# Summing four of six conditioning vectors on GpSimd instead of VectorE

## The chip, the core and the metric

The kernel runs on one core of a Trainium2 chip. A core has TensorE (matrix products, into PSUM), VectorE and ScalarE (elementwise work on SBUF and PSUM), GpSimd (elementwise work on SBUF alone) and SyncE, whose queue SP issues the loads and stores. Each engine runs its own instructions in order and waits for the others by semaphores. The metric is the device time of one execution in microseconds (us), as the median of several runs; lower is better.

## What is computed

One decoder block over 256 tokens of width 2048 in float32, conditioned on one vector c. Six vectors of 2048 numbers come from c by one product with a weight of 2048 x 12288 (100 MB, which is loaded once); the rest of the block uses them as shifts, scales and gates:

```python
c_act = jax.nn.silu(c)
mod = c_act @ w_ada[l] + b_ada[l]
sh_m, sc_m, gt_m, sh_f, sc_f, gt_f = [m[:, None, :] for m in jnp.split(mod, 6, axis=-1)]
h = rmsnorm(x, g[0]) * (1.0 + sc_m) + sh_m
y = token_mixer(h, w_in[l], ...)          # retention and S5 branches, merged by gates, times w_out
x = x + gt_m * rmsnorm(y, g[1])
h = rmsnorm(x, g[2]) * (1.0 + sc_f) + sh_f
y = swiglu_ffn(h, w_ffn_in[l], w_ffn_out[l])
x = x + gt_f * rmsnorm(y, g[3])
```

## The kernel before

**The weight stream.** Every large product goes through `linear`: it walks over pieces of 256 rows by 512 columns of a weight. For each piece SP loads a tile `raw` (L268, 512 KB), ScalarE rounds it to `hi` (L271), VectorE subtracts to get `lo` (the helper `tt`, L80), and TensorE makes twelve matmuls of 512 columns from it (L283, L284, L287: two token tiles, three products, two k-tiles). `raw` has a ring of five buffers (`RB`), `hi` and `lo` have three each. Results are evacuated some pieces later (`defer`).

**The conditioning vectors.** `ada_acc` makes one half of a vector (1024 columns): it loads 16 tiles `araw` of 128 x 1024 and sums them, each times its own element of `cT`, into a tile `acc`: the first by a scaling (L198), the others by a multiply and add in one VectorE instruction (L200). A matmul then sums over the partitions. `acc` has one buffer. The two vectors that the first stretch needs, SC_M and SH_M, are made with `first=True` and take their tiles from a pool of their own, `firstp`. The other four are SC_F and SH_F (`ada_f`, needed by the feed forward), GT_M (`ada_gm`) and GT_F (through `ada_rows`). Their `araw` tiles come from the ring of `raw`, which they share with the weights, but for GT_M, which has five buffers of its own (`lraw`).

**The order.** These sums are generators in a lane, `ada`; after each weight piece `tick` advances the lane by its rate (0.35 pieces' worth, then 0.5 for SC_F and SH_F, 0.8 for GT_M, 0.7 for GT_F). A second lane, `mix`, advances the retention heads and the S5 part in the same way. A scheduler in the language's tile framework may still move an instruction a little within its engine's row. In the profile, SC_F and SH_F are summed from 237 to 733 us, GT_M from 735 to 852, GT_F from 1401 to 1549; the feed forward's first product lies in between.

**GpSimd** has little to do before: memsets, and small powers (`rstd_of`, L140) for norms: `grs` in each retention head, which VectorE's `gnb` (L797) waits for, `rstd` and `rpost` in the other norms. Each S5 group has a small memset of `mg` (L677).

Of the kernel before, what the change touches and what calls it, by code (L numbers as in the profile page):

```python
# [15 lines left out]
ALU = mybir.AluOpType  # L16
# [36 lines left out]
def hybrid_block(ctx: ExitStack, tc: tile.TileContext, A, out, dbg=None):  # L53
# [7 lines left out]
    x_in, w_ada, w_in = A["x"], A["w_ada"], A["w_in"]  # L61
    w_ret, w_glu, w_out, w_f1, w_f2 = A["w_ret_out"], A["w_s5_glu"], A["w_out"], A["w_ffn_in"], A["w_ffn_out"]
    V, S, G, T = nc.vector, nc.scalar, nc.gpsimd, nc.tensor
# [26 lines left out]

# [1 line left out]
    class Lane:  # L92
# [34 lines left out]

# [1 line left out]
    ident = cst.tile([P, P], F32, name="ident")  # L129
# [27 lines left out]
    cT = cst.tile([P, KD], F32, name="cT")  # L157
# [18 lines left out]

# [1 line left out]
    mod = cst.tile([P, 96], F32, name="mod")  # L178
# [8 lines left out]
    def ada_acc(col, n, first=False):  # L187
        acc = adp.tile([P, n], F32, tag="acc", name="acc")
        for kt in range(KD):
# [6 lines left out]
            nc.sync.dma_start(raw, w_ada[kt * P:(kt + 1) * P, col:col + n])  # L196
            if kt == 0:
                V.tensor_scalar(acc, raw, cT[:, 0:1], None, op0=ALU.mult)  # L198
            else:
                V.scalar_tensor_tensor(acc, raw, cT[:, kt:kt + 1], acc, op0=ALU.mult, op1=ALU.add)  # L200
            yield acc
# [62 lines left out]

# [1 line left out]
    def split_piece(w, k0, KP, c0, keep=None, kept=None, tag="hi", hi=None):  # L266
# [94 lines left out]

# [1 line left out]
    def square_sum(a, o):  # L363
# [39 lines left out]

# [1 line left out]
    NS = 32  # L405
# [119 lines left out]

# [1 line left out]
    eye = cst.tile([P, 32], F32, name="eye")  # L527
# [219 lines left out]

# [1 line left out]
    ret = []  # L749
# [51 lines left out]

# [1 line left out]
    KG = [(0, 4), (4, 10), (10, 16)]  # L803
# [113 lines left out]

# [1 line left out]
    flush()  # L919
# [53 lines left out]

# [1 line left out]
    def out_evac(pst, t, n, Y, ssq, Gr, squared=False):  # L975
# [91 lines left out]

# [1 line left out]
    h2 = lhs_of(h2_t)  # L1069
# [87 lines left out]
```

## Time and profile before

| | |
|---|---|
| median of 3 runs | 1674.71 us (1673.17 to 1676.5) |
| span of the profiled execution, first to last instruction | 1672.3 us |
| TensorE matmul busy | 1622.4 us, 97% |
| VectorE busy | 1167.2 us, 70% |
| ScalarE busy | 800.0 us, 48% |
| GpSimd busy | 19.0 us, 1% |
| moved by DMA | 398.14 MB, 238 GB/s |

The profile comes from one execution, of 1672.3 us; the median lies 2.4 us above that span. Busy shares are averages over stretches with different limits, so the stretches in which the four vectors are summed have to be read each by itself. In the rows below PE is TensorE's matmuls, PEld its weight loads, DVE is VectorE, ACT ScalarE, POOL GpSimd, and SPq SyncE's queue; L200 is line 200 of the kernel. An arrow `<-` in a name stands between what an instruction writes and what it reads, and behind a time it names what ended a wait. A tile named `ps_` or `mm` lies in PSUM, the others in SBUF.

### The profile page before, as it was taken

The numbers are of one execution on the slowest core, as the hardware profiler recorded it, in microseconds if no ns is written. First come the engines' busy times: TensorE is split into PE (matmuls) and PEld (weight loads), VectorE is DVE, ScalarE is ACT, GpSimd is POOL, SyncE is SP. The second block draws the span as 40 slices with busy tenths as digits, with TensorE's granted clock in tenths as the row PEclk, the third lists the DMA queues.
The fourth block names the chain that finished last, engine by engine and source line by source line (L and its number), as shares of the span: only waits on it lengthen the run. The fifth ranks groups of instructions, "written<-read, shape, count | busy, mean of one in ns | idle before, by whom it ended". The sixth has DMA issues, their size and how long they took to land.

```text
span 1672.3 us, 20673 instructions
## 1 busy us (share of the span) xinstructions
PE 1622.4 (97%) x7531; PEld 1317.4 (79%) x7531; DVE 1167.2 (70%) x1570; ACT 800.0 (48%) x1102; POOL 19.0 (1%) x39
## 2 busy tenths in 40 slices
PE   5999999999999999999998999999999999999997
PEld 2778887888888888888886788888888888778786
DVE  7878887888878997779967544444444445667554
ACT  4454448454656465544456544444444444334442
POOL 0000000010000000000000000000000000000000
PEclk9999999999999999999999999999999999999999
DMA  9999976865766867799985666666666667889763
GB/s 353 335 316 323 324 236 184 261 198 181 248 222 203 264 205 238 262 317 325 332 282 180 189 188 188 189 189 187 187 187 185 188 189 220 270 284 328 252 190 126
DMA packets 194094, 398.14 MB, mean 238 GB/s; under 512 B 23128, under 2 KB 24488, under 8 KB 193480
## 3 DMA queue, kind: packets, MB, share of 16 engines
q1 hardware_dynamic: 193928, 396.74, 73.7%
q8 instruction: 59, 0.97, 0.2%
q14 instruction: 43, 0.35, 0.1%
q0 software_dynamic: 64, 0.08, 0.0%
HBM read 394.67 MB, written 2.10 MB: 237 GB/s over the span
## 4 chain that ended last, share of the span: by engine, by line
PE 83%; DMA 6%; DVE 5%; ACT 3%; issue 2%; POOL 0%; DVEq 0%; SPq 0%; POOLq 0%; ACTq 0%
PE mm L283 26%; PE mm L287 26%; PE mm L284 26%; DMA araw<-in_w_ada_dram 4%; DVE lo L80 2%; ACT hi L271 1%; DVE acc L200 1%; ACT uS L821 1%; PE ps_v L664 1%; PE ps_ada L183 1%; PE ps_y L709 1%; DMA fraw<-in_w_ada_dram 1%; DMA raw<-in_w_ffn_in_dram 1%; PE ps_a L1090 1%; PE ps_bt L657 0%
## 5 line engine op out<-in xcount | busy, mean ns | idle before, releaser
L271 ACT ACTIVATE hi<-raw 128x1024 fp32r<-128x1024 f32 x539 | 568.4, 1059 | 693.1 <-PE mm L284 581.9
L80 DVE TENSOR_TENSOR lo<-raw,hi 128x1024 fp32r<-128x1024 f32 x519 | 632.2, 1222 | 357.8 <-ACT hi L271 354.1
L283 PE MATMUL mm<-hi,h 128*128 128x512 f32 x1408 | 561.4, 399 | 3.7 <-ACT hi L271 3.4
L284 PE MATMUL mm<-hi,h 128*128 128x512 f32 x1408 | 554.2, 394 | 1.8 <-DVE h L80 1.8
L287 PE MATMUL mm<-lo,h 128*128 128x512 f32 x1376 | 429.4, 393 | 0.8 <-DVE lo L80 0.8
L283 PEld LDWEIGHTS mm<-hi,h 128*128 128x128 f32 x1408 | 266.6, 189 | 61.6 <-ACT hi L271 4.1
L284 PEld LDWEIGHTS mm<-hi,h 128*128 128x128 f32 x1408 | 266.4, 189 | 58.4 <-DVE h L80 2.5
L287 PEld LDWEIGHTS mm<-lo,h 128*128 128x128 f32 x1376 | 258.9, 189 | 61.2 <-DVE lo L80 3.5
L200 DVE SCALAR_TENSOR_TENSOR acc<-araw,cT,acc 128x1024 f32<-128x1024 f32 (+1 forms) x180 | 214.3, 1190 | 58.7 <-DMA araw<-in_w_ada_dram 58.2
L283 PE MATMUL mm<-hi,aT 128*128 128x512 f32 x348 | 136.5, 392 | 0.1
L284 PE MATMUL mm<-hi,aT 128*128 128x512 f32 x348 | 136.4, 392 | 0.0
L287 PE MATMUL mm<-lo,aT 128*128 128x512 f32 x348 | 110.1, 395 | 6.4 <-DVE lo L80 6.3
L287 PEld LDWEIGHTS mm<-lo,aT 128*128 128x128 f32 x348 | 64.3, 188 | 24.4 <-DVE lo L80 11.1
L283 PEld LDWEIGHTS mm<-hi,aT 128*128 128x128 f32 x348 | 65.4, 188 | 15.2 <-ACT hi L271 0.8
L284 PEld LDWEIGHTS mm<-hi,aT 128*128 128x128 f32 x348 | 65.4, 188 | 14.0
L283 PE MATMUL mm<-hi,rT 128*128 128x512 f32 x128 | 51.0, 399 | 0.6 <-ACT hi L271 0.6
L283 PE MATMUL mm<-hi,yg 128*128 128x512 f32 x128 | 50.5, 395 | 0.0
L284 PE MATMUL mm<-hi,mT 128*128 128x512 f32 x128 | 50.5, 394 | 0.0
L284 PE MATMUL mm<-hi,rT 128*128 128x512 f32 x128 | 50.4, 394 | 0.0
L283 PE MATMUL mm<-hi,mT 128*128 128x512 f32 x128 | 50.2, 393 | 0.0
L284 PE MATMUL mm<-hi,yg 128*128 128x512 f32 x128 | 50.1, 391 | 0.0
L287 PE MATMUL mm<-lo,rT 128*128 128x512 f32 x128 | 39.9, 393 | 0.1
(258 smaller groups left out, 1259.5 us busy)
## 6 DMA issues: line engine op xcount, KB each, us to landing
raw<-in_w_ffn_in_dram SPq DMA_DIRECT2D x178, 512.0 KB, 3.7
raw<-in_w_in_dram SPq DMA_DIRECT2D x176, 512.0 KB, 4.7
araw<-in_w_ada_dram SPq DMA_DIRECT2D x128, 512.0 KB, 5.2
raw<-in_w_ffn_out_dram SPq DMA_DIRECT2D x88, 512.0 KB, 5.4
araw<-in_w_ada_dram SPq DMA_DIRECT2D x64, 384.0 KB, 5.6
raw<-in_w_out_dram SPq DMA_DIRECT2D x34, 512.0 KB, 5.8
raw<-in_w_ret_out_dram SPq DMA_DIRECT2D x32, 512.0 KB, 5.1
raw<-in_w_s_glu_dram SPq DMA_DIRECT2D x32, 512.0 KB, 5.0
```

Of the source, the lines that this page charges most:

```text
L80: V.tensor_tensor(o, a, b, op=op)
L183: T.matmul(ps[:, i:i + 1], acc[:, i * P:(i + 1) * P], ones[:, 0:1], start=True, stop=True)
L200: V.scalar_tensor_tensor(acc, raw, cT[:, kt:kt + 1], acc, op0=ALU.mult, op1=ALU.add)
L271: S.activation(hi, raw, AF.Copy)
L283: T.matmul(pst[t], xh, hi[:, k, :], start=kt == ka, stop=False)
L284: T.matmul(pst[t], xl, hi[:, k, :], start=False, stop=False)
L287: T.matmul(pst[t], xh, lo[:, k, :], start=False, stop=kt == kb - 1)
L664: T.matmul(pv[:, o:o + 64], BT[:, ri, t, :], uS[0][:, 4 * e + t, :], start=True, stop=True)
L709: T.matmul(o, X[:, ri, t, :], mat(CB, ri, t), start=ri == 0, stop=False, tile_position=(0, 64 * v))
L821: S.activation(dst, src, AF.Copy)
L1090: T.transpose(ps[:, j * P:(j + 1) * P], act[t][:, j * P:(j + 1) * P], ident)
```

## The change

In `ada_acc`, the accumulations with `first=True` stay on VectorE. In all other calls GpSimd does the work: the first tile is scaled into `acc` by GpSimd, and each further tile is scaled in place by GpSimd and then added to `acc` by a second GpSimd instruction. Comments elsewhere are dropped, with nothing else changed; behind the edit every line number is higher by 5.

```diff
@@ ada_acc
             nc.sync.dma_start(raw, w_ada[kt * P:(kt + 1) * P, col:col + n])
-            if kt == 0:
+            if first and kt:
+                V.scalar_tensor_tensor(acc, raw, cT[:, kt:kt + 1], acc, op0=ALU.mult, op1=ALU.add)
+            elif first:
                 V.tensor_scalar(acc, raw, cT[:, 0:1], None, op0=ALU.mult)
+            elif kt:
+                G.tensor_scalar(raw, raw, cT[:, kt:kt + 1], None, op0=ALU.mult)
+                G.tensor_tensor(acc, acc, raw, op=ALU.add)
             else:
-                V.scalar_tensor_tensor(acc, raw, cT[:, kt:kt + 1], acc, op0=ALU.mult, op1=ALU.add)
+                G.tensor_scalar(acc, raw, cT[:, 0:1], None, op0=ALU.mult)
             yield acc
```

VectorE's row at the first half of GT_M, before: splits `lo` of the weight stream, the gated unit's products `gl`, and the accumulations `acc`.

```order
L80 TENSOR_TENSOR lo_6618<-raw_6614,hi_6616 128x1024
L200 SCALAR_TENSOR_TENSOR acc_6585<-araw_6607,cT_105,acc_6585 128x1024
L80 TENSOR_TENSOR lo_6643<-raw_6639,hi_6641 128x1024
L200 SCALAR_TENSOR_TENSOR acc_6585<-araw_6632,cT_105,acc_6585 128x1024
L200 SCALAR_TENSOR_TENSOR acc_6585<-araw_6675,cT_105,acc_6585 128x1024
L80 TENSOR_TENSOR lo_6661<-raw_6657,hi_6659 128x1024
L200 SCALAR_TENSOR_TENSOR acc_6585<-araw_6696,cT_105,acc_6585 128x1024
L80 TENSOR_TENSOR lo_6682<-raw_6678,hi_6680 128x1024
```

The same place of VectorE's row in the change.

```order
L80 TENSOR_TENSOR lo_6679<-raw_6675,hi_6677 128x1024
L80 TENSOR_TENSOR lo_6705<-raw_6701,hi_6703 128x1024
L80 TENSOR_TENSOR lo_6723<-raw_6719,hi_6721 128x1024
L80 TENSOR_TENSOR gl_6509<-gl_6509,mm_6597 128x512
L80 TENSOR_TENSOR gl_6510<-gl_6510,mm_6598 128x512
L80 TENSOR_TENSOR lo_6745<-raw_6741,hi_6743 128x1024
```

The accumulations are gone from it; the splits and the gated unit's products follow each other as before.

GpSimd's row at the same place of the change. Before, nothing stood there: the last `mg` and the next norm's `rpost` followed each other.

```order
L202 TENSOR_SCALAR araw_6667<-araw_6667,cT_105 128x1024
L202 TENSOR_SCALAR araw_6693<-araw_6693,cT_105 128x1024
L202 TENSOR_SCALAR araw_6737<-araw_6737,cT_105 128x1024
L202 TENSOR_SCALAR araw_6759<-araw_6759,cT_105 128x1024
L205 TENSOR_SCALAR acc_6645<-araw_6646,cT_105 128x1024
L203 TENSOR_TENSOR acc_6645<-acc_6645,araw_6667 128x1024
L203 TENSOR_TENSOR acc_6645<-acc_6645,araw_6693 128x1024
L203 TENSOR_TENSOR acc_6645<-acc_6645,araw_6737 128x1024
L203 TENSOR_TENSOR acc_6645<-acc_6645,araw_6759 128x1024
L202 TENSOR_SCALAR araw_6799<-araw_6799,cT_105 128x1024
L203 TENSOR_TENSOR acc_6645<-acc_6645,araw_6799 128x1024
```

Two passes per loaded tile stand there now; at the head of the half four scalings come ahead of the first write of `acc`, which has to wait until the half before has been read.

GpSimd's row at the first retention heads, before: the powers `grs` of the group norms follow each other.

```order
L140 TENSOR_TENSOR grs_2894<-rst_2895,mhalf_89 128x2
L140 TENSOR_TENSOR grs_2981<-rst_2982,mhalf_89 128x2
L140 TENSOR_TENSOR grs_3009<-rst_3010,mhalf_89 128x2
L140 TENSOR_TENSOR grs_3035<-rst_3036,mhalf_89 128x2
L140 TENSOR_TENSOR grs_3103<-rst_3104,mhalf_89 128x2
```

And the same place in the change.

```order
L202 TENSOR_SCALAR araw_3140<-araw_3140,cT_105 128x1024
L203 TENSOR_TENSOR acc_2116<-acc_2116,araw_3140 128x1024
L140 TENSOR_TENSOR grs_2904<-rst_2905,mhalf_89 128x2
L202 TENSOR_SCALAR araw_3254<-araw_3254,cT_105 128x1024
L203 TENSOR_TENSOR acc_2116<-acc_2116,araw_3254 128x1024
L140 TENSOR_TENSOR grs_2992<-rst_2993,mhalf_89 128x2
L202 TENSOR_SCALAR araw_3314<-araw_3314,cT_105 128x1024
L203 TENSOR_TENSOR acc_2116<-acc_2116,araw_3314 128x1024
L140 TENSOR_TENSOR grs_3020<-rst_3021,mhalf_89 128x2
```

A scaling and an add now stand ahead of a power, and the power waits in the same row for them and for their tile's load.

## Rows read from the trace of the kernel before

**Rows 1.** The page, part 1: busy us, share of the span, instructions.

```profile
PE 1622.4 (97%) x7531; PEld 1317.4 (79%) x7531; DVE 1167.2 (70%) x1570; ACT 800.0 (48%) x1102; POOL 19.0 (1%) x39
```

**Rows 2.** The page, part 4: the chain that ended last, by line.

```profile
PE mm L283 26%; PE mm L287 26%; PE mm L284 26%; DMA araw<-in_w_ada_dram 4%; DVE lo L80 2%; ACT hi L271 1%; DVE acc L200 1%; ACT uS L821 1%; PE ps_v L664 1%; PE ps_ada L183 1%; PE ps_y L709 1%; DMA fraw<-in_w_ada_dram 1%; DMA raw<-in_w_ffn_in_dram 1%; PE ps_a L1090 1%; PE ps_bt L657 0%
```

**Rows 3.** Windows, four stretches: busy us (instructions) by engine, clock, DMA share, GB/s.

```profile
236.00:403.00 167.00, 161.55 (x753) 132.88 (x752) 137.12 (x246) 94.06 (x128) 9.36 (x14) 0.99 0.67 208
403.00:733.00 330.00, 328.70 (x1755) 269.89 (x1754) 275.73 (x428) 190.57 (x353) 0.74 (x7) 1.00 0.75 243
735.00:852.00 117.00, 117.00 (x530) 96.42 (x530) 107.30 (x109) 52.33 (x61) 0.00 (x0) 1.00 0.93 323
1409.00:1550.00 141.00, 135.06 (x584) 107.78 (x583) 97.54 (x86) 56.30 (x63) 0.00 (x0) 1.00 0.87 291
```

**Rows 4.** Waits, 1405 to 1558: us in total, times, longest us.

```profile
PE mm L287 <- DVE lo L80: 5.8, 6, 2.4
```

**Rows 5.** VectorE by line, 735 to 852: xcount | busy us, mean ns | idle before.

```profile
L80 DVE TENSOR_TENSOR lo<-raw,hi 128x1024 fp32r<-128x1024 f32 x40 | 48.7, 1221 | 5.7 <-ACT hi L271 5.6
...
L200 DVE SCALAR_TENSOR_TENSOR acc<-araw,cT,acc 128x1024 f32<-128x1024 f32 x30 | 38.4, 1279 | 0.9 <-DMA araw<-in_w_ada_dram 0.8
...
L80 DVE TENSOR_TENSOR gl<-gl,M 128x512 f32<-128x512 f32 x8 | 5.2, 683 | 0.0
...
L80 DVE TENSOR_TENSOR gl<-gl,Sg 128x512 f32<-128x512 f32 x6 | 3.9, 685 | 0.0
...
L198 DVE TENSOR_SCALAR acc<-araw,cT 128x1024 f32<-128x1024 f32 x2 | 1.5, 746 | 0.0
```

**Rows 6.** VectorE by line, 1409 to 1550.

```profile
L80 DVE TENSOR_TENSOR lo<-raw,hi 128x1024 fp32r<-128x1024 f32 x47 | 57.0, 1222 | 17.3 <-ACT hi L271 17.3
...
L200 DVE SCALAR_TENSOR_TENSOR acc<-araw,cT,acc 128x1024 f32<-128x1024 f32 x29 | 37.2, 1281 | 23.2 <-DMA araw<-in_w_ada_dram 23.0
...
L198 DVE TENSOR_SCALAR acc<-araw,cT 128x1024 f32<-128x1024 f32 x1 | 0.8, 752 | 1.6 <-DMA araw<-in_w_ada_dram 1.6
```

**Rows 7.** VectorE by line, 403 to 733.

```profile
L80 DVE TENSOR_TENSOR lo<-raw,hi 128x1024 fp32r<-128x1024 f32 x100 | 121.2, 1219 | 17.4 <-ACT hi L271 17.3
...
L200 DVE SCALAR_TENSOR_TENSOR acc<-araw,cT,acc 128x1024 f32<-128x1024 f32 x45 | 57.6, 1280 | 28.6 <-DMA araw<-in_w_ada_dram 28.5
...
L80 DVE TENSOR_TENSOR q<-bs,lam 128x256 f32<-128x256 f32 x32 | 12.2, 418 | 0.1
...
L198 DVE TENSOR_SCALAR acc<-araw,cT 128x1024 f32<-128x1024 f32 x3 | 2.2, 745 | 0.0
...
L606 DVE SCALAR_TENSOR_TENSOR cn<-par 128x16 f32<-128x16 f32 x1 | 0.2, 168 | 0.0
```

**Rows 8.** GpSimd by line, whole span.

```profile
L623 POOL MEMSET CB<- 128x1024 f32 x1 | 1.0, 951 | 0.0
...
masks.py:199 POOL TENSOR_SCALAR_AFFINE_SELECT ident<-ident 128x128 f32<-128x128 f32 x1 | 0.3, 296 | 0.0
...
masks.py:197 POOL MEMSET ident<- 128x128 f32 x1 | 0.2, 205 | 0.3 <-POOLq L1143 0.3
```

**Rows 9.** Timeline: start us, us, engine, instruction [idle before <- releaser]; three places.

```profile
357.37 0.68 DVE L80 TENSOR_TENSOR rT<-ps_r,rT 128x512 fp32r<-128x512 f32 x1
357.63 0.69 POOL L140 TENSOR_TENSOR grs<-rst,mhalf 128x2 f32<-128x2 f32 x1 [3.50 <-DVE rst L139]
...
894.72 0.56 POOL L140 TENSOR_TENSOR rpost<-rst,mhalf 128x1 f32<-128x1 f32 x1 [246.24 <-DVE rst L139]
895.31 1.41 DVE L1033 SCALAR_TENSOR_TENSOR x<-Y,rpost,x 128x512 f32<-128x512 f32 x2 [0.67 <-POOL rpost L140]
...
910.83 1.22 DVE L80 TENSOR_TENSOR flo<-raw,hi 128x1024 fp32r<-128x1024 f32 x1
910.99 1.46 POOL L140 TENSOR_TENSOR rpost<-rst,mhalf 128x1 f32<-128x1 f32 x1 [10.85 <-DVE rst L139]
```

**Rows 10.** The page, part 6: DMA issues, KB each, median us to landing.

```profile
araw<-in_w_ada_dram SPq DMA_DIRECT2D x128, 512.0 KB, 5.2
```

## Prediction

> **What bounds the kernel now.** I read the busy shares first: TensorE is busy 97% of the span, VectorE 70%, GpSimd 1% [rows 1]. Then the chain that ended last: three matmul lines hold about 26% each, VectorE's split L80 2%, its accumulation L200 1% [rows 2]. So the matmul stream bounds the kernel nearly everywhere, and VectorE's accumulations are mostly hidden. What the change can win is TensorE's idle time in the stretches where the four vectors are summed. The table of windows gives it [rows 3]: 5.45 us (167 - 161.55) in 236 to 403, 1.3 us in 403 to 733, nothing in 735 to 852, 5.94 us in 1409 to 1550; 12.7 us in all. Only a part of that is VectorE's: in the last stretch the matmuls on lo waited 5.8 us in all for VectorE's split [rows 4].
>
> So the gain is capped at about 6 to 12 us, and the question is whether GpSimd can do the work in the time that each stretch leaves.
>
> **What is removed and added.** By the code eight sums of 16 accumulations leave VectorE: 120 of L200 at 1.28 us and 8 of L198 at 0.75 us [rows 5 to 7], 160 us in all. They stand in four stretches: 48 (45 + 3) in 403 to 733 [rows 7], 32 (30 + 2) in 735 to 852 [rows 5], 30 (29 + 1) in 1409 to 1550 and two just before it [rows 6], and the other 16 in 236 to 403. GpSimd gets two passes over a 128x1024 tile in place of each, a scaling in place and an add that reads two tiles; the add waits for the scaling. I call the pair a step. The time that a stretch has for a step, from its length and its count: 10.4 us in the first, then 6.9, 3.66 and 4.7 us.
>
> **What a step costs.** No row shows either pass at this size. The nearest are GpSimd's memsets: 951 ns for 1024 columns, 205 ns for 128, which makes 0.83 ns a column and 0.1 us fixed; and the select over 128 columns, which also reads its tile, 296 ns, so 91 ns more per 128 columns, 0.73 us per 1024 [rows 8]. Lower bound: each pass is as cheap as a memset, 1.9 us. Upper bound: every read is paid on top, 0.95 + 0.73 for the scaling and 0.95 + 2 x 0.73 for the add, 4.1 us. I choose the memset for the scaling (one tile in, one out) and the row that reads for the add, whose two reads must come through: 0.95 + 2.41 = 3.36 us. The Trainium skill, "GPSIMD Engine Reference", section on performance versus the Vector engine, gives 4497 ns for such an add of 2048 columns; half of that, 2.25 us, is an estimate from that page, and by it the sum below would lose 0.16 us a step, at most 18 us over the 110 steps of the three late stretches.
>
> **What the step meets.** GpSimd's tiny power, one column, takes 0.56 us when VectorE is idle. Started 0.16 us into a VectorE split that reads two SBUF tiles it took 1.46 us, and ended 0.40 us after the split did; started beside a VectorE subtraction that reads one tile from PSUM, it took 0.69 us for two columns [rows 9]. So GpSimd waits for a VectorE instruction with two SBUF inputs, for the whole of it. The Trainium skill, "SBUF", practical consequences of the port table, has the rule: such a pair excludes each other for the full instruction, in either order. The trace agrees for the order seen here; no row shows a long GpSimd read with VectorE behind it. By that rule alone the sum is the full one below; without any exclusion it would be nil.
>
> The VectorE work that stays and reads two SBUF tiles, by stretch: in 735 to 852, lo 48.7, gl with M 5.2 and with Sg 3.9, 57.8 us [rows 5]; in 1409 to 1550, lo 57.0 [rows 6]; in 403 to 733, lo 121.2 and 36 groups of the S5 part from 12.2 down to 0.2 us, 232 instructions and 94.9 us, together 216 [rows 7].
>
> If nothing overlaps, a stretch needs that work plus its steps:
> 735 to 852: 57.8 + 32 x 3.36 = 165.3, against 117: 48 us over. The late ring has five buffers, so GpSimd may lag by five steps less one landing and one step before SP's queue stops: 5 x 3.66 - 5.2 - 3.36 = 9.7 us (landing from [rows 10]). 38 us are left.
> 403 to 733: 216 + 48 x 3.36 = 377, against 330: 47 us.
> 1409 to 1550: 57.0 + 30 x 3.36 = 157.8, against 141: 17 us. The ring here is shared with the weights, so no slack is taken off.
> 236 to 403 has 10.4 us for each step and is taken as free.
> Sum 102 us.
>
> If only the streaming excludes and each instruction's fixed part overlaps, less is lost. From 1221 ns for 1024 columns and about 684 for 512 [rows 5], 0.15 us of a VectorE instruction is fixed; of a GpSimd pass 0.1 us. In 735 to 852: 54 and 64 instructions, 8.1 + 6.4 us off, 24 us left. In 403 to 733: 332 and 96, 49.8 + 9.6 off, 318 us, which fits in 330: nothing. In 1409 to 1550: 47 and 60, 7.1 + 6 off, 4 us. Sum 28 us. I take the middle of 28 and 102, 65 us, less the 2 us or so of waits on lo that VectorE's relief may win back: 63.
>
> **How it reaches the end.** A GpSimd pass that waits holds the next scaling behind it, and with it the araw buffer. SP issues in order, so the next araw load that finds no buffer stops the weight loads behind it; then ScalarE's and VectorE's splits and the matmuls run dry. A split that waits behind an add is late by up to 2.4 us, and its raw buffer with it. No transfer is added: the araw and weight loads are as many as before. The power instructions of the retention (grs) and the memsets of S5 (mg) now stand in GpSimd's row behind steps, as the rows of the program's order show; VectorE's gnb waits for grs. Eight of them, each behind at most one step, are 27 us of VectorE's time at most in 236 to 403, where it is busy 137 of 167 us now [rows 3] and 117 after; I take nothing, since that leaves 50 us idle, and the splits may run three pieces ahead of the matmuls; the price is up to 27 if that cover is gone.
>
> **The rivals.** First, **hidden**: GpSimd's passes overlap VectorE, every step fits (3.36 is below 3.66, the tightest period), nothing is slower and the freed VectorE gives little: 1671 to 1678 us. For it: GpSimd is idle 99% [rows 1]. Against it: the power under the split [rows 9].
>
> Second, **relief** (faster): with accumulations gone, the split comes sooner wherever TensorE waited for it, mostly in 1409 to 1550, where VectorE stands idle 23.2 us before accumulations for araw to land and the split behind them waits too [rows 6]. Price: 6 us there and up to 6 in 236 to 403, 1663 to 1669 us. It decides only if a step under exclusion costs less than (117 + 9.7 - 57.8) / 32 = 2.15 us; the lower bound of 1.9 is below that.
>
> Third, **dear steps**: the upper bound of 4.1 us with full exclusion. 735 to 852: 57.8 + 131.2 - 117 - 9 = 63; 403 to 733: 216 + 196.8 - 330 = 83; 1409 to 1550: 57 + 123 - 141 = 39; sum 185, 1860 us.
>
> Fourth, **the shared ring** alone, without exclusion: in 1409 to 1550 a buffer comes round every 5 x 141 / 77 = 9.2 us (30 accumulations and 47 splits), and an araw tile would hold it 5.2 + 3.36 = 8.6 us. It does not bind by itself, 0 to 5 us, and ends with "hidden".
>
> **How the numbers follow.** The profiled span is 1672.3 us; the median of the runs is 1674.7, so 2.4 us lie around the span. 1672.3 + 63 + 2.4 gives 1738 us. Chances: the forecast (exclusion, 10 to 135 us lost) 0.66; dear steps, or the GpSimd row held up by grs and mg besides, 0.12; hidden 0.12; relief 0.10. About 0.2%, 3.3 us, is what a measurement of this kernel can tell from no change. Of "hidden", 0.11 fall within it and 0.01 below; so faster 0.11, same 0.11, slower 0.78. The range reaches from "hidden" and a part of "relief", 1666, to 1812, which leaves out the dear steps and the rest of relief, some 0.2.
>
> **What would show it.** Right: in the changed kernel's stretches of the GT_M vector and of the S5 part GpSimd is busy most of the time, an add takes well over 2.4 us where it meets a split, lo takes longer than 1.22 us or starts late, SP's loads wait for GpSimd, and TensorE has idle time where it now has none. The first 236 us and the feed-forward part between 950 and 1400 us stay as they are. Wrong: adds of less than 1.5 us, or adds and splits that overlap without stretching; then the time stays or falls. If the loss is in 236 to 403 instead, it is grs and not the port.

## The result, and the profile after

The changed kernel takes 1990.21 us (median of 4 runs, 1986.8 to 1993.27) against 1675.61 us (1673.17 to 1677.5, 4 runs) before: a ratio of 1.1876, 95% interval 1.1855 to 1.1897. The forecast was 1738, with 1812 as its upper end. The direction was right; the loss, 314 us, is five times the 63 that were forecast.

The page of the changed kernel, part 1, the row of TensorE's granted clock in part 2, and the chain of part 4 (before: [rows 1, 2]):

```profile
PE 1728.5 (87%) x7531; PEld 1368.2 (69%) x7531; DVE 1172.6 (59%) x1442; ACT 799.7 (40%) x1102; POOL 767.3 (39%) x287
...
PEclk9999998898989889889978899999999999888999
...
PE 31%; POOL 23%; DMA 10%; DVE 4%; issue 2%; ACT 1%; SPq 0%; POOLq 0%; DVEq 0%; ACTq 0%
```

GpSimd now holds 23% of the chain that ended last, and loads 10%; before, no GpSimd line stood in it. VectorE lost 128 instructions and is busy as long as before: what remains takes longer. TensorE's 7531 matmuls are busy 106 us longer (1728.5 against 1622.4), and TensorE idles 207 us more (257.3 against 49.9).

Where that happens, windows of the changed kernel (columns as in [rows 3]): the retention heads, the end of the S5 part, the sums of GT_M, and the feed forward:

```profile
236.00:403.00 167.00, 128.45 (x539) 102.28 (x538) 104.12 (x138) 69.86 (x92) 86.47 (x32) 0.90 0.49 168
735.00:900.00 165.00, 135.23 (x632) 105.09 (x631) 99.21 (x108) 67.83 (x128) 108.75 (x38) 0.90 0.51 178
900.00:1050.00 150.00, 116.06 (x487) 90.37 (x486) 99.89 (x76) 49.66 (x57) 148.28 (x49) 0.89 0.69 239
1200.00:1650.00 450.00, 450.00 (x2009) 370.20 (x2008) 221.12 (x201) 189.68 (x201) 0.00 (x0) 1.00 0.65 188
```

The last column but two is the granted clock, a mean between its two levels of 1.2 and 2.4 GHz: 0.89 to 0.90 where TensorE has gaps, 1.00 where it has none. In the feed forward nothing changed. In GT_M GpSimd is busy 148 of 150 us; in the two stretches ahead of it only 52% and 66%, and TensorE starves there as well. Those need another reason than a full row.

The costliest groups of part 5 that answer to the step, in the changed kernel (lines are 5 higher):

```profile
L80 DVE TENSOR_TENSOR lo<-raw,hi 128x1024 fp32r<-128x1024 f32 x519 | 702.2, 1357 | 655.8 <-ACT hi L276 645.7
...
L202 POOL TENSOR_SCALAR araw<-araw,cT 128x1024 f32<-128x1024 f32 x120 | 406.9, 3392 | 284.4 <-DMA araw<-in_w_ada_dram 200.1
...
L203 POOL TENSOR_TENSOR acc<-acc,araw 128x1024 f32<-128x1024 f32 x120 | 314.9, 2624 | 9.8
```

A step is 3.39 + 2.62 = 6.0 us, and GpSimd stood idle 200 us for araw tiles that had not landed. The waits of SP's queue in the changed kernel say why they were late (line waited for: us in total, times, longest):

```profile
SPq L196 <- POOL acc L203: 331.8, 54, 10.9
SPq L273 <- POOL acc L203: 321.1, 43, 10.6
```

653 us of loads waited for GpSimd to release a buffer, those of araw (L196) and of weights (L273) alike. One turn of that, SP's queue and then GpSimd, in the changed kernel's S5 part:

```profile
646.14 0.42 SPq L196 DMA_DIRECT2D araw<-in_w_ada_dram  x1
646.65 1.06 SPq L273 DMA_DIRECT2D raw<-in_w_ret_out_dram  x2
658.60 0.34 SPq L196 DMA_DIRECT2D araw<-in_w_ada_dram  x1
```
```profile
651.69 3.87 POOL L202 TENSOR_SCALAR araw<-araw,cT 128x1024 f32<-128x1024 f32 x1 [6.04 <-DMA araw<-in_w_ada_dram]
655.64 2.92 POOL L203 TENSOR_TENSOR acc<-acc,araw 128x1024 f32<-128x1024 f32 x1
662.41 2.85 POOL L202 TENSOR_SCALAR araw<-araw,cT 128x1024 f32<-128x1024 f32 x1 [3.84 <-DMA araw<-in_w_ada_dram]
```

The load issued at 646.14 is there at 651.69; the step ends at 658.56; and at 658.60, not earlier, SP issues the next araw load. GpSimd then idles until that one has landed. So 12.5 us go by for one araw and two weight pieces; SP's queue, which is in order, issues nothing more until 658.60.

To place the loss I take from each trace the first matmul on a split of the gated unit's products `yg`, the first on one of the feed forward's `aT`, and the end of the span. Up to the first lie the sums of SC_F and SH_F, between the two those of GT_M, behind the second those of GT_F. The rows (min/median/max ns, first and last start), before and then after:

```profile
L287 PE MATMUL mm<-lo,aT x348: 388/392/503, 1410.8 to 1663.1; 128*128 128x512 f32 x174
...
L287 PE MATMUL mm<-lo,yg x128: 388/392/397, 720.6 to 812.7; 128*128 128x512 f32 x128
```
```profile
L292 PE MATMUL mm<-lo,aT x348: 387/394/792, 1661.1 to 1976.6; 128*128 128x512 f32 x174
...
L292 PE MATMUL mm<-lo,yg x128: 388/392/796, 899.6 to 1035.2; 128*128 128x512 f32 x128
```

So the loss is 179.0 us with SC_F and SH_F, 71.3 with GT_M (761.5 against 690.2) and 63.2 with GT_F (324.7 against 261.5); together 313.5, the difference of the spans. The same three differences, in us, for the runs below that sum the vectors where the change does; the last column is the time of one run each, but for the change, where it is the median of four. Beside them the kernel before took 1675.1 to 1676.6 us.

| run | SC_F, SH_F | GT_M | GT_F | time |
|---|---|---|---|---|
| the change | 179.0 | 71.3 | 63.2 | 1990.21 |
| e2_shadow | 7.2 | 52.2 | 1.9 | 1735.32 |
| e3_hold | 55.4 | 87.9 | 58.0 | 1875.35 |
| e6_actscale | 79.9 | 32.1 | 14.4 | 1800.62 |
| e7_bcast | 130.4 | 64.1 | 52.9 | 1921.53 |
| e8_noadd | 209.8 | 71.3 | 74.3 | 2029.51 |
| e9_offqueue | 180.2 | 76.2 | 66.1 | 1996.61 |
| e12_write | 8.6 | 40.3 | 24.6 | 1747.55 |
| e14_turns | 155.1 | 72.9 | 56.5 | 1958.55 |
| e15_turns_before | 4.7 | 1.6 | 0.2 | 1680.94 |
| e16_split | 114.6 | 67.4 | 55.8 | 1911.84 |
| e17_split_before | 10.4 | 2.1 | 20.1 | 1707.04 |
| e20_hold_after | 25.9 | 47.7 | 35.7 | 1783.36 |
| e21_hold_split | 32.0 | 39.5 | 35.1 | 1780.65 |

### The profile page after: what moved, and what is told of

Same layout as the page of the kernel before. It is cut to its first block, busy times and chain, and to the rows that moved or that the text cites. A ratio compares the mean times of both kernels' runs of the same rounds, so it can differ in the third digit from the quotient of the medians.

```text
span 1985.8 us, 20782 instructions
## 1 busy us (share of the span) xinstructions
PE 1728.5 (87%) x7531; PEld 1368.2 (69%) x7531; DVE 1172.6 (59%) x1442; ACT 799.7 (40%) x1102; POOL 767.3 (39%) x287
## 4 chain that ended last, share of the span: by engine, by line
PE 31%; POOL 23%; DMA 10%; DVE 4%; issue 2%; ACT 1%; SPq 0%; POOLq 0%; DVEq 0%; ACTq 0%
POOL araw L202 12%; PE mm L288 10%; PE mm L289 10%; PE mm L292 10%; POOL acc L203 10%; DMA araw<-in_w_ada_dram 6%; DMA raw<-in_w_ret_out_dram 2%; DVE lo L80 1%; ACT hi L276 1%; DMA raw<-in_w_ffn_out_dram 1%; POOL acc L205 1%; DMA raw<-in_w_in_dram 1%; DMA raw<-in_w_out_dram 1%; DVE q L80 1%; DMA raw<-in_w_ffn_in_dram 0%
## 5 line engine op out<-in xcount | busy, mean ns | idle before, releaser
L80 DVE TENSOR_TENSOR lo<-raw,hi 128x1024 fp32r<-128x1024 f32 x519 | 702.2, 1357 | 655.8 <-ACT hi L276 645.7
L288 PE MATMUL mm<-hi,h 128*128 128x512 f32 x1408 | 573.2, 407 | 33.1 <-ACT hi L276 32.5
L289 PE MATMUL mm<-hi,h 128*128 128x512 f32 x1408 | 564.0, 401 | 1.7 <-DVE h L80 1.7
L202 POOL TENSOR_SCALAR araw<-araw,cT 128x1024 f32<-128x1024 f32 x120 | 406.9, 3392 | 284.4 <-DMA araw<-in_w_ada_dram 200.1
L203 POOL TENSOR_TENSOR acc<-acc,araw 128x1024 f32<-128x1024 f32 x120 | 314.9, 2624 | 9.8
L205 POOL TENSOR_SCALAR acc<-araw,cT 128x1024 f32<-128x1024 f32 x8 | 29.4, 3675 | 671.0 <-DMA araw<-in_w_ada_dram 486.2
L288 PE MATMUL mm<-hi,aT 128*128 128x512 f32 x348 | 146.1, 420 | 34.1 <-ACT hi L276 34.0
L289 PE MATMUL mm<-hi,aT 128*128 128x512 f32 x348 | 143.4, 412 | 0.0
L288 PE MATMUL mm<-hi,rT 128*128 128x512 f32 x128 | 56.9, 445 | 23.3 <-ACT hi L276 23.2
L288 PE MATMUL mm<-hi,yg 128*128 128x512 f32 x128 | 53.6, 418 | 9.3 <-ACT hi L276 9.3
L198 DVE SCALAR_TENSOR_TENSOR acc<-araw,cT,acc 128x768 f32<-128x768 f32 x60 | 60.9, 1015 | 0.4 <-DMA araw<-in_w_ada_dram 0.2
L288 PE MATMUL mm<-hi,mT 128*128 128x512 f32 x128 | 51.4, 401 | 4.2 <-ACT hi L276 4.2
```

What stands on the lines that cost most here:

```text
L80: V.tensor_tensor(o, a, b, op=op)
L202: G.tensor_scalar(raw, raw, cT[:, kt:kt + 1], None, op0=ALU.mult)
L203: G.tensor_tensor(acc, acc, raw, op=ALU.add)
L205: G.tensor_scalar(acc, raw, cT[:, 0:1], None, op0=ALU.mult)
L288: T.matmul(pst[t], xh, hi[:, k, :], start=kt == ka, stop=False)
L289: T.matmul(pst[t], xl, hi[:, k, :], start=False, stop=False)
```

## The experiments

### What the two passes cost, alone and beside VectorE

The kernel before, with work appended behind its last store: each pass alone, then GpSimd passes and VectorE sums of two SBUF tiles started together.

```diff
+    for n in (1024, 1024, 512, 256):
+        G.tensor_scalar(ga[:, 0:n], ga[:, 0:n], cT[:, 0:1], None, op0=ALU.mult)
...
+        G.tensor_tensor(ga[:, 0:n], ga[:, 0:n], gb[:, 0:n], op=ALU.add)
...
+    for _ in range(8):
+        G.tensor_tensor(ga, ga, gb, op=ALU.add)
+    for _ in range(16):
+        tt(va, va, vb, ALU.add)
```

> The kernel before, with GpSimd passes on dead tiles appended behind the output: first alone, then eight at a time beside VectorE instructions. Its total time is longer by the appended work and says nothing. Theory A (a pass is dear by itself): the scaling of 128x1024 by a per-partition scalar takes about 2.8 us alone, the add about 2.3 us, as the shortest ones in the changed kernel did. Theory B (the passes are stretched by VectorE): alone they take 1.0 to 1.7 us and reach 2.8 only beside VectorE. On exclusion: eight adds beside sixteen VectorE sums of two SBUF tiles (1.22 us each) take 8 x 2.34 + 16 x 1.22 = 38 us together if they exclude each other, 19.5 us if they overlap; beside sums with one PSUM tile, and memsets beside sums of two SBUF tiles, they overlap.

The timeline of GpSimd in that run (start, us): scaling by a column and by a constant, add, multiply by a broadcast column, copy, memset; then 8 adds beside 16 VectorE sums, 8 scalings beside 16 sums, 8 adds beside 32 VectorE sums with a PSUM operand:

```profile
1675.16 2.85 POOL L1141 TENSOR_SCALAR Y<-Y,cT 128x1024 f32<-128x1024 f32 x1
1678.09 2.77 POOL L1142 TENSOR_SCALAR Y<-Y 128x1024 f32<-128x1024 f32 x1
...
1683.88 2.34 POOL L1144 TENSOR_TENSOR Y<-Y 128x1024 f32<-128x1024 f32 x1
1686.30 1.89 POOL L1145 TENSOR_TENSOR Y<-Y,cT 128x1024 f32<-128x1024 f32 x1
1688.25 1.04 POOL L1146 COPY Y<-Y 128x1024 f32<-128x1024 f32 x1
1689.35 0.95 POOL L1147 MEMSET Y<- 128x1024 f32 x1
...
1730.80 26.33 POOL L1153 TENSOR_TENSOR Y<-Y 128x1024 f32<-128x1024 f32 x8
...
1767.62 27.07 POOL L1158 TENSOR_SCALAR Y<-Y,cT 128x1024 f32<-128x1024 f32 x8
...
1795.46 19.33 POOL L1163 TENSOR_TENSOR Y<-Y 128x1024 f32<-128x1024 f32 x8
```

And VectorE's: 8 sums alone, 16 beside the adds, 16 beside the scalings:

```profile
1720.18 10.04 DVE L80 TENSOR_TENSOR Y<-Y 128x1024 f32<-128x1024 f32 x8 [0.28 <-POOL Y L1137]
...
1730.75 36.27 DVE L80 TENSOR_TENSOR Y<-Y 128x1024 f32<-128x1024 f32 x16 [0.28 <-POOL Y L1137]
...
1767.56 26.48 DVE L80 TENSOR_TENSOR Y<-Y 128x1024 f32<-128x1024 f32 x16 [0.28 <-POOL Y L1137]
```

The add is as I had it (2.34 for 2.41; the estimate from the Trainium skill, "GPSIMD Engine Reference", section on performance versus the Vector engine, 2.25, agrees), the scaling three times as dear (2.85 for 0.95): 5.2 us a step. Adds and VectorE's sums shut each other out: 36.27 us, where one after the other would be 18.7 + 20.1. Scalings hardly do: 26.48, not 42.9, some 0.8 us of VectorE's time for each scaling. The rule that I took from the Trainium skill, "SBUF", practical consequences of the port table, thus holds here for the add; for the scaling, which also reads SBUF, the measurement shows no such full exclusion, and decides.

### The port alone, and the hold alone

In `e2_shadow` VectorE keeps all its sums; beside 20 of GT_M's 32 accumulations GpSimd scales and adds a tile that nobody needs. No load of a weight or of an araw tile waits for it.

```diff
+                V.tensor_copy(go, acc[:, 0:1])
+                G.tensor_scalar(scr, scr, go, None, op0=ALU.mult)
+                G.tensor_tensor(scr, scr, scr, op=ALU.add)
```

> The kernel before; VectorE still sums everything, and in the GT_M stretch GpSimd does 20 steps (scaling and add) on a tile of its own, started by a small VectorE copy after the accumulation. No load waits for GpSimd. Theory of the port (GpSimd and VectorE exclude each other): 20 steps of 5.2 us are 104 us, VectorE's two-tile work there is 96 us, the stretch of 117 us grows by 20 to 80 us. Theory of the held buffers: VectorE and GpSimd may wait for each other, but nothing on the path does, and the total grows by less than 10 us.

It took 1735.32 us, 59 more than before: with VectorE's sums still there (107 of 117 us busy, [rows 3]) the passes cost it time that it does not have: the matmuls wait there for VectorE's `lo` and `gl`. Of the 52 us lost with GT_M some 10 have another reason: at the end of the stretch a load of `x` waited 11.7 us for GpSimd's last pass, with the weight loads behind it in SP's queue, and TensorE stood idle 9.9 us in one piece. The rest, some 40 us, lies in the range that I had for the port (20 to 80): where VectorE is full, the port is real.

In `e3_hold` VectorE keeps all its sums too, and GpSimd holds each araw buffer without reading more than two columns of it.

```diff
+            if not first:
+                G.tensor_copy(scr[:, 0:1], raw[:, 0:1])
+                for _ in range(16 if kt else 9):
+                    G.memset(scr, 0.0)
+                G.tensor_copy(scr[:, 0:1], raw[:, 1:2])
```

> The kernel before; VectorE still sums everything, and GpSimd reads one column of each araw tile of the four vectors, then writes 16 memsets of 256 columns (about 5 us, the price of a step) and reads one column again. So every araw buffer is held as long as a GpSimd step holds it, and GpSimd's row is as full, but no long GpSimd read meets VectorE. Theory of the held buffers: 150 to 310 us of the 314 lost come back. Theory of the port: less than 60 us.

1875.35 us, 199 more than before. The small memsets were paced at 0.37 us each, so that the hold came to some 7.2 us and not 6. VectorE's split takes 1223 ns as before, so nothing held it up: holding a buffer and filling GpSimd's row is dear without any contention.

### Another step in the same places

Three kernels change what a step is and leave its place: by their traces SP issues its 793 loads in the order of the change, but for 17 places in `e6_actscale`. ScalarE scales and GpSimd adds:

```diff
-                G.tensor_scalar(raw, raw, cT[:, kt:kt + 1], None, op0=ALU.mult)
+                S.activation(raw, raw, AF.Copy, scale=cT[:, kt:kt + 1])
```

> The changed kernel with the scaling done by ScalarE (1.06 us for such a tile) in place of GpSimd; the add stays on GpSimd. If the price of the scaling pass on GpSimd (2.8 us and more) is the main cost, a step there falls to 2.4 to 2.9 us, below every stretch's period, and the time falls to 1680 to 1760 us. If the meeting of adds and splits is the main cost, more than half of the loss stays: above 1830 us.

GpSimd multiplies by a broadcast column instead of scaling:

```diff
-                G.tensor_scalar(raw, raw, cT[:, kt:kt + 1], None, op0=ALU.mult)
+                G.tensor_tensor(raw, raw, cT[:, kt:kt + 1].to_broadcast([P, n]), op=ALU.mult)
```

> The changed kernel with the scaling written as a GpSimd multiply by the element of cT broadcast along the row (1.89 us alone, against 2.85 us); the sums are the same. A step alone falls from 5.2 to 4.2 us. Price of the step and held buffers: the loss falls by a fifth to a third, 1880 to 1930 us. Port: the multiply reads two tiles and excludes VectorE fully, which the scaling hardly did (in the first experiment eight scalings cost VectorE 6.4 us, eight adds 16 us), so little is won: above 1950 us.

GpSimd scales twice and adds nothing:

```diff
-                G.tensor_tensor(acc, acc, raw, op=ALU.add)
+                G.tensor_scalar(acc, raw, cT[:, kt:kt + 1], None, op0=ALU.mult)
```

> The changed kernel with the GpSimd add replaced by a second scaling of araw into acc; this leaves out the sum over the rows, so the four vectors are wrong. A step alone is 5.7 us, longer than 5.2, but neither pass excludes VectorE for its whole length. Held buffers: as slow or slower, 1960 to 2050 us. Port: much of the loss goes, below 1880 us.

The rows of the two passes by line, in `e7_bcast` and in `e8_noadd`:

```profile
L203 POOL TENSOR_TENSOR acc<-acc,araw 128x1024 f32<-128x1024 f32 x120 | 347.6, 2897 | 9.3
L202 POOL TENSOR_TENSOR araw<-araw,cT 128x1024 f32<-128x1024 f32 x120 | 296.7, 2474 | 302.2 <-DMA araw<-in_w_ada_dram 199.8 <-DVE spill L80 18.9 <-DVE q L80 17.7
```
```profile
L203 POOL TENSOR_SCALAR acc<-araw,cT 128x1024 f32<-128x1024 f32 x120 | 379.4, 3162 | 11.0
L202 POOL TENSOR_SCALAR araw<-araw,cT 128x1024 f32<-128x1024 f32 x120 | 378.9, 3159 | 288.3 <-DMA araw<-in_w_ada_dram 197.4 <-issue 40.2 <-DVE sc L263 11.1
```

And VectorE's split in both, which shows how much it was held up:

```profile
L80 DVE TENSOR_TENSOR lo<-raw,hi 128x1024 fp32r<-128x1024 f32 x519 | 810.5, 1571 | 478.3 <-ACT hi L276 472.9 <-PE mm L292 4.1 <-PE ps_ada L183 0.3
```
```profile
L80 DVE TENSOR_TENSOR lo<-raw,hi 128x1024 fp32r<-128x1024 f32 x519 | 653.7, 1262 | 782.8 <-ACT hi L276 777.0 <-PE mm L289 3.9
```

This is the row of experiments that decides most. In order of the step's length (`e6_actscale` 1.15 + 2.56 on its two engines, `e7_bcast` 5.37, the change 6.02, `e8_noadd` 6.32 us) the time rises at every point: +124, +245, +314, +353. What VectorE suffers goes another way: in the same order its split takes 1453, 1571, 1357 and 1262 ns. Were VectorE's lost time the cause, `e7_bcast` would be the slowest and `e8_noadd` the fastest of them. It is nearly the other way round, and VectorE's whole busy time says the same (1185, 1330, 1173 and 1075 us). So among these four kernels, which issue their loads in one order, the loss goes with the length of the step, that is with how long a buffer is held and GpSimd's row occupied, and not with what VectorE suffers. The times of `e7_bcast` and `e8_noadd` are those that I expected if price and held buffers count; that of `e6_actscale` lies between my two ranges (to 1760, from 1830).

### GpSimd's queue, and an early release

> The changed kernel with the small memset of mg in each S5 group moved from GpSimd to VectorE, so that nothing of S5 stands behind the steps in GpSimd's row. Theory of the queue (S5 waits for memsets that stand behind steps, and steps behind memsets that wait for S5): 30 to 100 us come back. If only price, buffers and port count: within 15 us of the changed kernel.

`e9_offqueue` moves the S5 part's memset `mg` from GpSimd to VectorE (`V.memset` for `G.memset`, one line). 1996.61 us: no gain. That a step stands behind an `mg` costs nothing.

> The changed kernel with each step but the first of a half replaced by one-column reads of araw around 13 memsets of 256 columns, about 6 us like a step of the changed kernel, and a one-column write of acc; this leaves out the sums. VectorE has lost its accumulations as in the change, buffers are held as long, GpSimd's row is as full, but no long GpSimd read meets VectorE. Held buffers and price: the loss stays, 1920 to 2000 us. Port: most of it goes, below 1800 us.

`e12_write` was meant to hold buffers without reads, by the same memsets between two one-column copies, of which the second wrote `acc`. The scheduler put both copies ahead of the 13 memsets, so that each buffer was released as soon as GpSimd came to it. So its time, which lies in the range of "port", decides nothing between the two. It tells something else: with GpSimd's row filled by 5 to 6 us for every tile, but no buffer held for a step and no long read, SC_F and SH_F lose only 8.6 us instead of 179. The 40 us of GT_M stay: there the row itself is too long.

### Which buffer waits

The framework chooses a tile's buffer in the ring when the program is built. In the changed kernel it gave 23 of 48 araw tiles of the S5 part one that an araw had held before. `e14_turns` and its control `e15_turns_before` take the five in turn:

```diff
+    turn = iter(range(10000))
...
-                raw = wp.tile([P, n], F32, tag="raw", name="araw", bufs=RB)
+                raw = wp.tile([P, n], F32, tag=f"raw{next(turn) % RB}", name="araw", bufs=1)
```

> The changed kernel with one thing different: the five buffers of the ring that weights and araw tiles share are now taken strictly in turn. In the changed kernel as it was, the program gave 23 of 48 araw tiles of the S5 stretch a buffer that an earlier araw had held, so that the load of one waits until GpSimd is done with the other (landing 5.5, scaling and add 6 to 6.8: some 12 us a round, with weights queued behind it); in turn it is 2 of 48. In the gate of the feed forward it goes the other way, 24 araw loads behind GpSimd and 5 weight loads, where it was 15 and 14. Theory 'araw behind araw': the loss up to the gated unit's products falls from 179 us to about 55 to 90, the part of the middle gate stays near 72, that of the last gate 40 to 80; the whole 1845 to 1915. Rival 'price and port' (the passes are as dear, and meet VectorE as often, whichever buffer they work on): 1960 to 2000.

> Control: the kernel before, with the ring's five buffers taken strictly in turn. Both theories: 1668 to 1690, since VectorE holds a buffer for 1.28 us only, whichever it is. Over 1700 would mean that the order of buffers matters by itself, and the result of its partner is to be read against this one.

1958.55 and 1680.94 us. 24 us come back in the S5 part, not 90 to 125: my theory of "araw behind araw" was too narrow, and the whole lies just below the rival's 1960 to 2000. Up to the gated unit's products no araw load waits for a step any more (in the change there are 21 such waits). Now it is the weight loads that wait for GpSimd (414 us in 56 waits), and the next araw load stands behind them in SP's queue.

Three buffers for the weights and two for araw, in the change and in the kernel before:

```diff
+        k = int(sums and own[0])
+        turn[k] += 1
+        if k:
+            return f"raw{3 + turn[1] % (RB - 3)}"
+        return f"raw{turn[0] % (3 if own[0] else RB)}"
```

> The changed kernel, with the five shared buffers divided while SC_F, SH_F and GT_F are summed: three for the weights, two for araw, each taken in turn. GpSimd's passes, their prices and VectorE's work are the same; but no weight load waits for GpSimd's buffer any more, and an araw load waits for the one before the last, so that its landing (5.5 us) lies beside the step of the one between (6). Theory 'held ring': against the control with the same division, the loss up to the gated unit's products falls from 179 us to 40 or less, the middle gate's part stays near 72 (GpSimd's row is full there: 32 x 6.0 = 192 us for a stretch of 117), the last gate's falls to 30 to 45 (192 against 150): 100 to 155 us over the control, 1780 to 1850. Rival 'port and price' (VectorE stands behind the passes, whoever holds which buffer): the loss up to the gated unit's products stays over 120 us, and the whole is 230 us or more over the control, over 1900.

> Control: the kernel before, with the same division into three and two buffers in the same stretches. Three weight buffers at 3.1 us a piece give 9.3 us for a landing of 5.2, ScalarE's 1.06 and VectorE's 1.22: it should nearly hold, 1672 to 1720 by both theories.

1911.84 and 1707.04 us; against this control the loss is 104.2 with SC_F and SH_F, 65.3 with GT_M, 35.7 with GT_F. The two gates came as the theory of the held ring had it; the first part fell between the theories (40 or less, over 120), and so did the whole, 204.8 us over the control (100 to 155, 230 or more).

### Time enough for each step

Only GT_F is summed by GpSimd here, and its sums are spread over the feed forward, one araw after five weight pieces:

```diff
+    Gf = []
+    gf = ada.add(ada_rows(GT_F, 3, Gf))
+    ada.rate = 0.2
     for n in range(11):
...
-    Gf = []
-    gf = ada.add(ada_rows(GT_F, 3, Gf))
-    ada.rate = 0.7
```

> A candidate: only the last gate's vector is summed by GpSimd, and it is summed during the feed forward, one araw after every five weight pieces, where the last stretch needs none; the other three stay on VectorE. Theory 'a step must fit the time between two araw loads': a step of 6 us has some 15 us, and of its araw loads 1 of 32 waits for GpSimd (30 weight loads do, five tiles after it, 12 us, against 11.2 us of landing and step): 1662 to 1685. Rival 'port and held buffers cost wherever GpSimd sums': 30 adds each hold up a split, and 30 weight loads: 1700 to 1740.

> Control of the candidate: the kernel before with the last gate's sums moved into the feed forward in the same way, but left on VectorE. TensorE's idle 5.9 us of the last stretch come back, and the feed forward has VectorE time to spare: 1666 to 1676 by both theories. Against its partner it shows what GpSimd's part of that move is worth.

On GpSimd 1707.3 us, ratio 1.019 to before (1.0156 to 1.0225); on VectorE 1667.95 us, ratio 0.994 (0.9918 to 0.9961), which beats both kernels of this study. The feed forward from 950 to 1450 us, first with GpSimd, then with VectorE (columns as in [rows 3]), and in the first SP's longest wait and TensorE's:

```profile
950.00:1450.00 500.00, 480.99 (x2084) 386.99 (x2083) 255.97 (x217) 196.26 (x208) 162.62 (x57) 0.99 0.60 210
```
```profile
950.00:1450.00 500.00, 500.00 (x2231) 411.80 (x2230) 283.75 (x260) 211.20 (x222) 0.00 (x0) 1.00 0.72 221
```
```profile
SPq L274 <- POOL acc L204: 240.4, 28, 11.0
...
PE mm L289 <- ACT hi L277: 18.3, 11, 3.3
```

VectorE is busy half of the time and GpSimd a third, and still TensorE stands idle 19 us and has 147 matmuls fewer in the same 500 us: once for each step the fifth load behind an araw waits 8.6 us in the mean until GpSimd is done, and the ring of five runs empty. TensorE's idle time was ended by ScalarE's `hi`, and `hi` waited 162.4 us in 62 waits for weights to land, where the control has no such wait. VectorE's splits are stretched too (1362 ns in this window, 1225 in the control), but TensorE waited for none of them here. So this is the held buffer by itself, without a full row. The 1707 us lie in the rival's range (1700 to 1740) and not in that of my theory (1662 to 1685): that landing and step, 11.2 us, fit the 12 us until the buffer's next load was not enough.

The same with four buffers for the weights and one for araw:

> The last gate's vector summed by GpSimd during the feed forward, one araw after five weight pieces (1707 us when all shared five buffers, 39 us over the same move on VectorE), now with four buffers for the weights and one for araw. GpSimd's passes are the same, and its step and landing, 11.2 us, fit the 14.75 us between two araw loads. Theory 'held ring': the 39 us go, within 10 us of the control on VectorE with the same division, 1666 to 1690. Rival 'port and price': 25 to 40 us over that control remain, 1695 to 1720.

> Control: the same early sums on VectorE, with the same four and one buffers in the feed forward. Four weight buffers at 2.95 us a piece give 11.8 us against some 8 that a piece needs: 1665 to 1685 by both theories.

1783.97 and 1680.66 us: worse by 103, and both theories missed it. With a buffer of their own the scheduler moved the araw loads forward in SP's queue, to one after every two weight loads. Each then waited for the one buffer (223.7 us in 28 waits), with the weight loads behind it in the queue. The control issues its loads in much the same order and loses nothing like it. A single buffer of its own does not help where the queue is shared and in order.

### The reads taken away

GpSimd's two passes are replaced by the hold of `e3_hold` (two one-column copies, both into `scr`, around 13 memsets), once in the change and once with the divided ring:

```diff
-                G.tensor_scalar(raw, raw, cT[:, kt:kt + 1], None, op0=ALU.mult)
-                G.tensor_tensor(acc, acc, raw, op=ALU.add)
+                G.tensor_copy(scr[:, 0:1], raw[:, 0:1])
+                for _ in range(13):
+                    G.memset(scr, 0.0)
+                G.tensor_copy(scr[:, 0:1], raw[:, 1:2])
```

> The four sums are left out; in place of scaling and add GpSimd reads one column of the araw tile, writes 13 small memsets to a tile of its own (estimate from the memsets paced at 0.37 us in an earlier run: 4.8, with the two column reads some 6 us), and reads one more column. The buffer is held as long as by the changed kernel's step and GpSimd's row is as full, but no long pass reads a tile, so nothing is there that could hold up VectorE. The buffers fall much as in the run that took them in turn: 2 of 48 araw loads behind an araw, 43 weight loads. That run lost 155 us up to the gated unit's products. Theory 'held ring': that stays, 120 us or more, and the whole 1890 to 1960. Rival 'port' (long passes against VectorE's two-tile instructions): 60 us or less there, GT_M still some 65 from its full row, the whole 1780 to 1840.

> The same replacement (sums left out, one-column reads around 13 memsets) in the kernel with three buffers for the weights and two for araw, whose partner with GpSimd's real passes took 1911.84 us and lost 104 us against its control up to the gated unit's products. Theory 'held ring' (here: araw loads that wait in SP's row with weights behind them): 80 us or more of the 104 remain, the whole 1880 to 1920. Rival 'port': 40 us or less remain there, the whole 1800 to 1850.

1783.36 and 1780.65 us. With SC_F and SH_F 25.9 us are lost, and 21.6 against the control of the divided ring. That is what "port" expected. But the step is some 5.7 us here (4.76 for the memsets, 0.40 and 0.36 for the copies, the rest between them) and 6.0 there, and the scheduler also laid the loads out more evenly (two or three weight loads between araw loads, where `e14_turns` has them in pairs and `e16_split` in bursts). So more than one thing changed at once, and the pairs do not separate them. In windows of the same work, first `e14_turns`, then `e20_hold_after`, one sees both: VectorE busy 202 against 149 us, and DMA at 0.54 against 0.70. The third window is the same work in `e8_noadd`:

```profile
592.00:875.00 283.00, 240.37 (x1158) 192.47 (x1159) 201.99 (x257) 119.54 (x224) 183.30 (x64) 0.89 0.54 180
```
```profile
530.00:746.00 216.00, 213.43 (x1157) 176.51 (x1156) 148.54 (x251) 120.79 (x224) 143.57 (x429) 1.00 0.70 234
```
```profile
606.00:930.00 324.00, 254.71 (x1159) 198.78 (x1159) 164.56 (x254) 121.40 (x224) 208.63 (x68) 0.86 0.47 159
```

It speaks against VectorE's stretched work as the main reason. VectorE is busy 165 us there, only 16 more than in `e20_hold_after`, and the same matmuls take 324 us instead of 216. SP's loads stand in nearly the same order in both (34 of 793 places differ). What differs is the step, 6.3 against 5.7 us, and who waits for it: up to the gated unit's products araw loads waited 198.0 us in 22 waits for GpSimd's steps, much as in the change (186.0 in 21), and in `e20_hold_after` 55.6 us in 11.

## Why the prediction was wrong

**The bound and the direction.** That the matmul stream bounds the kernel, that the freed VectorE wins nothing and that the feed forward stays as it is came true. Relief and "hidden" did not occur; "dear steps", 1860 us, came nearest and is still 130 us short.

**The step of 3.36 us failed.** "I choose the memset for the scaling": GpSimd's scaling costs three memsets. The step is 5.2 us alone and 6.0 in the kernel, outside the bounds of 1.9 to 4.1. This alone breaks the GT_M term. In a sum of GpSimd's row alone, 32 x 6.02 = 193 us stand against 117, less a slack of 18.3 - 5.2 - 6.0 = 7: 69 us, and 71.3 were lost, with GpSimd busy 148 of 150 us. That the two lie so close is in part luck: the same sum gives 47 us for `e7_bcast` (64.1 lost), 78 for `e8_noadd` (71.3) and 58 for `e20_hold_after` (47.7). The 38 us came from exclusion at a wrong price.

**The exclusion was right for half a step.** Adds shut VectorE's two-tile work out, scalings hardly do. The passes in the kernel are 0.8 us a step longer than alone. With the true 5.2 us my full sum (57.8 + 166 - 117 - 8, 216 + 249 - 330, 57 + 156 - 141) would give 99 + 135 + 72 = 306 us, close to the 313.5. That agreement is a coincidence: its GT_M term is 28 us too large, it has nothing for the heads, and the series of three steps shows that the loss does not follow what VectorE suffers.

**"The shared ring ... does not bind by itself, 0 to 5 us" failed.** Landing and step are 5.2 + 6.0 = 11.2 us against 9.2 in which a buffer comes round in GT_F, and 11.1 (5 x 330 / 148) in the stretch of 403 to 733. I had 8.6, and did the comparison for GT_F alone. `e10_early_pool` shows the mechanism by itself. In `e12_write`, where buffers are released and the long reads are gone, 8.6 of the 179 us with SC_F and SH_F are left; in `e20_hold_after`, which has no long reads either but holds the buffers, 25.9. In `e16_split`, against a control that is itself 32 us slower than the kernel before, some 27 of the 63 us of GT_F and 75 of the 179 are gone with a divided ring.

**"236 to 403 ... is taken as free" failed.** TensorE is busy 128.45 of 167 us there and was 161.55 [rows 3]. A step fits its 10.4 us; the landing and the step in the ring do not. The `grs` that I took at nothing, up to 27 us, made `gnb` wait 30.0 us in 7 waits. ScalarE's `spill`, which reads `gnb`, waited 36.8 us, and up to 590 us TensorE waited 33.6 us for the heads' tiles `sT` and `spill` (17.1, 10.7 and 5.8). So some of the loss may run through `grs`, as the last sign of the prediction had it; in the same stretch SP's loads waited 227.4 us for GpSimd's adds, and no run separates the two. The same 1162 matmuls stand in 506 to 721 us before and in 590 to 900 us in the change: 84 of the 179 us had been lost ahead of them, 95 among them.

**Not in the sum at all:** TensorE's clock. Where it had gaps, waiting for splits, the granted clock fell from its upper level to the lower one for part of the time (the mean from 0.99 to 0.90 in 236 to 403, from 1.00 to 0.89 in GT_M), and a matmul on `yg` took up to 796 ns instead of 397. The busy time is 106 us more for the same 7531 matmuls, beside 207 us more of idle time. How much of it reaches the end was not tested.

**What stays open** is how much VectorE's stretched work adds in the S5 part where the ring is laid out otherwise. In the change's own layout `e8_noadd` loses most, 210 us, with VectorE's split stretched least. With real passes 155 and 104 us are lost there in two other layouts of the ring, without them 26 and 22; of these differences, 129 and 83 us, the load order has a part that no run separates. Also `e3_hold`, with a longer hold than the change, loses less there (55); by the program's order none of its 48 araw loads of the S5 part stands behind an araw, and by the trace its araw loads waited 13.4 us in 3 waits for GpSimd there.

## What to carry to other kernels

Before work is moved to another engine, time that very operation on it: a neighbour in the profile, a memset for a scaling, was off by three. Then compare landing plus hold with the time in which a buffer of the ring comes round, for every stretch. That they fit is needed and not enough: in `e10_early_pool` they did, 11.2 us against 12, and 39 us were lost, as I read it because the load that takes the freed buffer still has to land and be split before TensorE can use it. Where loads share one queue in order, one held buffer stops them all. A single buffer of its own made it worse (`e18_early_own`), two of five bought a part back (`e16_split`). Moving the last gate's sums to a stretch with spare time gained 0.6% on VectorE, which does them in one pass, and lost 1.9% on GpSimd; moving all four sums to the idle engine where they stood lost 19%.

## What the runs showed of the hardware

On 128x1024 float32 GpSimd's scaling takes 2.85 us, by a constant 2.77, out of place no less (2.84), while its add of two tiles takes 2.34, a multiply by a broadcast column 1.89, a copy 1.04. So a product with a column is cheaper as a two-tile multiply than as a scaling, though beside VectorE it took 2.47. GpSimd's adds beside VectorE sums with a PSUM operand took 19.33 us for 8 and were not held up; its scalings met VectorE's two-tile sums with far less loss than its adds, though beside VectorE's full row in `e2_shadow` a scaling took 4.03 us. GpSimd's memsets were not held up at all: 16 of 128x1024 beside 16 VectorE sums took 16.08 us, the sums 20.12.
